# A gate/up stage in which one product gets its own PSUM banks and the weight sums are made in smaller pieces

## The chip, the core and the metric

The kernel runs on one core of a Trainium2 chip. The metric is the device time of one execution in microseconds (us). Engines are named PE (matrix multiply), DVE (vector), ACT (scalar), POOL and SP (which issues most transfers).

## The reference, cut to what matters here

One transformer block on 512 tokens of width 2048, in float32: a normed input projection, three mixers (a delta-rule recurrence, a gated linear recurrence, chunked retention), an output projection with residual, and a gated feed-forward block. The change lies in the last of these:

```python
h = rms_norm(x, norm2_g[l])
x = x + (jax.nn.silu(h @ ffn_w_gate[l]) * (h @ ffn_w_up[l])) @ ffn_w_down[l]
return rms_norm(x, final_norm_g)
```

The inner width is 5632.

## The kernel before

Every float32 product is made of three passes: each operand is split into a high half and the rest, and `mm3` (L161) runs high·high, high·low and low·high (L162 to L164) into the same PSUM bank. `split` (L157) makes the two halves: ACT casts the high half (L158), DVE subtracts it from the raw value (L141, through `tt`) for the low half.

The kernel does the input projection and the mixers (to about 750 us), the output projection (to about 925), the gate/up stage (to about 1827) and the down projection (to the end). The normed activation lies in SBUF as split pieces (`form(...)`: HH, HL, FAH, FAL).

The gate/up stage runs 11 units (`gate_up`, L993 to L1059). A unit multiplies the activation with four blocks of weights, b11, b21, b12 and b22, each of two buffers of 128 x 2048 (b11 = RB0, RB1; b12 = RB2, RB3; b21 = RB4, RB5; b22 = RB6 and RAW), loaded on SP's queue (L998). It uses a scheme with seven products on sums of blocks in place of eight on blocks. A `product` (L1001) has four pieces of 1024 weight columns; a piece is split into one of three slots (WH/WL twice, a part of HH/HL once) and used by 12 matmuls of 128x512. The products go into pairs of PSUM banks: bA is banks 0 and 1, bB is 2 and 3, bC is 4 and 5. The order of a unit:

1. b11 into bA, copied to E; then b11 becomes b11 + b12
2. b21 added into bA, whose result goes through tanh to G; then b12 becomes b12 + b22
3. b12 (the sum) into bB
4. b11 (the sum) into bC; then b11 becomes b11 + b22
5. b11 (the new sum) into bA; then E, H and X are formed from bA, bB and bC on DVE, and b21 becomes b21 + b11
6. b21 (the sum) into bB, from which H is subtracted, and which goes through tanh
7. b22 added into bC; E and G are finished

Each sum is made by `block` (L1013): two DVE additions of 128x2048. Then 16 transposes (L1056) go through banks 6 and 7; ACT copies them out (L1058) and stores them to HBM (`hscr`, L1059) from its own queue. High priority (`hp_`) lets the scheduler place such work early, among the matmuls of the next unit.

The down projection loads those activations back (`load_h`, L1100, on SP's queue, L1105), splits them (GH, GLo), and loads its weights in pieces of 128x512 (`wpieces`, L1085, transfers at L1093) into the buffers RAW and RW2.

The order of the instructions on each engine comes from the tile scheduler, which follows the order of the program and the priorities; a transfer is issued when its buffer and its queue slot are free, in the order of its queue.

Of the kernel before, what the change touches and what calls it, by code (L numbers as in the profile page):

```python
# [12 lines left out]
AF = mybir.ActivationFunctionType  # L13
# [18 lines left out]
NU = DFF // 512  # L32
# [66 lines left out]
def hybrid_block(ctx: ExitStack, tc: tile.TileContext, A: dict, out: bass.AP, dbg=None):  # L99
    nc = tc.nc  # L100
    V, S, G, PE = nc.vector, nc.scalar, nc.gpsimd, nc.tensor
# [17 lines left out]
    bank = [pp.tile([128, 512], F32, name=f"bank{i}") for i in range(8)]  # L119
# [9 lines left out]
    hscr = dp.tile([NCT, 128, T], F32, name="hscr")  # L129

    def c(name):
        o, n = CO[name]
        return cst[:, o:o + n] if o < NC1 else cs2[:, o - NC1:o - NC1 + n]
# [6 lines left out]
    def tt(o, a, b, op, eng=None):  # L140
        (eng or V).tensor_tensor(out=o, in0=a, in1=b, op=op)  # L141
# [7 lines left out]
    def stt(o, a, s, b, op0, op1, **kw):  # L149
        V.scalar_tensor_tensor(out=o, in0=a, scalar=s, in1=b, op0=op0, op1=op1, **kw)  # L150

    def act(o, a, f, scale=1.0, bias=0.0, **kw):
        S.activation(out=o, in_=a, func=f, scale=scale, bias=bias, **kw)  # L153

    MUL, ADD, SUB, MAX, MIN = ALU.mult, ALU.add, ALU.subtract, ALU.max, ALU.min

    def split(raw, hi, lo):  # L157
        S.copy(out=hi, in_=raw)  # L158
        tt(lo, raw, hi.bitcast(F32), SUB)

    def mm3(o, wh, wl, xh, xl, first, last, **kw):  # L161
        PE.matmul(o, wh, xh, start=first, stop=False, **kw)  # L162
        PE.matmul(o, wh, xl, start=False, stop=False, **kw)  # L163
        PE.matmul(o, wl, xh, start=False, stop=last, **kw)  # L164
# [13 lines left out]
    def sl(i, n=1):  # L178
        i -= (i > 9) + (i > 33) + (i > 44)
        return M[:, i * 512:(i + n) * 512]  # L180
# [10 lines left out]
    def nxt(k, n):  # L191
        v = ring[k]
        ring[k] = (v + 1) % n
        return v
# [27 lines left out]
    def head_rsqrt_stat(sq, rhs, n, mmb, floor=None, eps=None, kn=None):  # L222
        nt = sq.shape[-1] // 128
        v, y, h, t = smalls(nt * n, kn)
        b = mmb()
        for i in range(nt):
            mm(b[:, i * n:(i + 1) * n], sq[:, i * 128:(i + 1) * 128], rhs)
        if eps is None:
            ts(v, b[:, 0:nt * n], floor, MAX)
        else:  # L230
            ts(v, b[:, 0:nt * n], eps, ADD)
        rsqrt(y, v, (h, t))
        return y
# [36 lines left out]
    def proj(name, j, between=None):  # L270
        idx = W_IDX[(name, j)]
        o = bank[1 if ring["cv"] else nxt("proj", 2)]
        for half in range(2):
            with tc.high_priority() if idx > 1 else ExitStack():
                r = RAW[:, nxt("raw", 2), :]
                nc.sync.dma_start(out=r, in_=A["w_in"][idx, half])
                pcs = []
                for u in range(2):
                    w = nxt("w", 4)
                    split(r[:, u * 512:(u + 1) * 512], WH[:, w, :], WL[:, w, :])  # L280
                    pcs.append(w)
            if half and between:
                between()
            for u in range(2):
                w = pcs[u]
                for kk in range(4):
                    k = half * 8 + u * 4 + kk
                    cs = slice(kk * 128, (kk + 1) * 128)
                    mm3(o, WH[:, w, cs], WL[:, w, cs], HH[:, k, :], HL[:, k, :], k == 0, k == KT - 1)
        return o  # L290

    tok = []
    first = proj("k", 0, lambda: tok.append(head_rsqrt_stat(acc, c("mD"), 1, mmb, eps=NORM_EPS)))
# [350 lines left out]
    xc, tr, ti, la, th, lt, gx, g2 = (sl(34 + i) for i in range(8))  # L644
# [262 lines left out]
    E_, H_, X_, G_ = (ap_.tile([128, 2, T], F32, name=n) for n in ("E", "H", "X2", "G1"))  # L907
# [3 lines left out]
    def form(hl, j):  # L911
        if j < NFA:
            return (FAH, FAL)[hl][:, j, :, :]
        i = (j - NFA) * 1792
        return (HH, HL)[hl].rearrange("p k t -> p (k t)")[:, i:i + 1792].rearrange("p (f t) -> p f t", f=7)

    def fslot(i):
        if i < 2:
            return tuple(w[:, 2 * i:2 * i + 2, :].rearrange("p a b -> p (a b)") for w in (WH, WL))
        return tuple(w.rearrange("p k t -> p (k t)")[:, 7168:8192] for w in (HH, HL))  # L920
# [30 lines left out]
    for n, (ct, q) in enumerate(O_PIECES):  # L951
# [10 lines left out]
        if q == 3:  # L962
            b, x1 = ob[ct]
# [22 lines left out]
    rh, r2h = drv[:, 0:4], drv[:, 4:8]  # L986
# [6 lines left out]
    def gate_up(u):  # L993
        b11, b21, b12, b22 = blocks
        with tc.high_priority():
            for t_, m, half in ((b11, 0, 0), (b21, 0, 1), (b12, 1, 0), (b22, 1, 1)):
                for i in range(2):
                    nc.sync.dma_start(out=t_[i], in_=A["w_gu"][u, m, half, i])  # L998
        bA, bB, bC = (bank[0], bank[1]), (bank[2], bank[3]), (bank[4], bank[5])

        def product(raw, f, bs, first):  # L1001
            for jj in range(4):
                wh, wl = fslot(nxt("fs", 3))
                with tc.high_priority():
                    split(raw[jj // 2][:, 1024 * (jj % 2):1024 * (jj % 2) + 1024], wh, wl)
                for t in range(2):
                    tk = slice(128 * t, 128 * t + 128)
                    for i in range(2):
                        j, cs = 2 * jj + i, slice(512 * i, 512 * i + 512)
                        mm3(bs[t], form(0, j)[:, f, tk], form(1, j)[:, f, tk], wh[:, cs], wl[:, cs],  # L1010
                            first and j == 0, j == 7, skip_group_check=not first)

        def block(o, a, b_):  # L1013
            with tc.high_priority():
                for i in range(2):
                    tt(o[i], a[i], b_[i], ADD)

        two = range(2)
        hp_ = tc.high_priority
        product(b11, 0, bA, True)  # L1020
        with hp_():
            for t in two:
                S.copy(out=E_[:, t, :], in_=bA[t])
        block(b11, b11, b12)
        product(b21, 1, bA, False)
        with hp_():
            for t in two:
                act(G_[:, t, :], bA[t], AF.Tanh, scale=rh[:, t:t + 1])
                stt(G_[:, t, :], G_[:, t, :], 1.0, bA[t], ADD, MUL)
        block(b12, b12, b22)  # L1030
        product(b12, 4, bB, True)
        product(b11, 3, bC, True)
        block(b11, b11, b22)
        product(b11, 5, bA, True)
        with hp_():
            for t in two:
                tt(E_[:, t, :], bA[t], E_[:, t, :], SUB)
                tt(H_[:, t, :], bB[t], E_[:, t, :], ADD)
                tt(X_[:, t, :], bC[t], H_[:, t, :], ADD)
        block(b21, b21, b11)  # L1040
        product(b21, 2, bB, True)
        with hp_():
            for t in two:
                tt(H_[:, t, :], bB[t], H_[:, t, :], SUB)
                act(bB[t], H_[:, t, :], AF.Tanh, scale=rh[:, 2 + t:3 + t])
                stt(H_[:, t, :], bB[t], 1.0, H_[:, t, :], ADD, MUL)
                stt(X_[:, t, :], H_[:, t, :], r2h[:, 2 + t:3 + t], X_[:, t, :], MUL, MUL)
        product(b22, 6, bC, False)
        with hp_():
            for t in two:  # L1050
                tt(E_[:, t, :], bC[t], E_[:, t, :], ADD)
                stt(G_[:, t, :], G_[:, t, :], r2h[:, t:t + 1], E_[:, t, :], MUL, MUL)
            for f in range(4):
                b = bank[6 + nxt("tr", 2)]
                for t in range(4):
                    PE.transpose(b[:, 128 * t:128 * t + 128], (G_, X_)[t // 2][:, t % 2, 128 * f:128 * f + 128], ident)  # L1056
                st = H_[:, nxt("st", 2), :]
                S.copy(out=st, in_=b)  # L1058
                S.dma_start(out=hscr[4 * u + f], in_=st)  # L1059

    for u in range(NU):
        gate_up(u)
# [37 lines left out]
    def load_h(ci, n):  # L1100
        for i, ct in enumerate(range(D_START[ci], D_START[ci] + n)):
            f = FT[:, nxt("ft", 4), :]
            slot = ct % NS
            with tc.high_priority():
                nc.sync.dma_start(out=f, in_=hscr[ct])  # L1105
                split(f, GH[slot], GLo[slot])

    def down(ci, n):
# [118 lines left out]
    def lastb():  # L1227
        return bank[nxt("last", 2)]

    load_h(0, CHUNKS[0])  # L1230
    for ci, n in enumerate(CHUNKS):
        if ci < len(CHUNKS) - 1:
# [118 lines left out]
```

## Time and profile before

| what | value |
|---|---|
| median of 3 runs | 2339.6 us (2338.05 to 2344.82) |
| profiled execution | 2344.13 us |
| its span | 2342.3 us |
| PE busy | 2270.9 us, 97% of the span |
| DVE busy | 1627.8 us, 69% |
| ACT busy | 1000.3 us, 43% |
| mean granted clock of the PE | 0.99 |
| chain of work that ended last | PE 82%, DVE 11%, issue 4%, ACT 2%, DMA 1% |

The span is the profiled program from its first to its last instruction; the time of the run is 1.8 us more. Matmuls overlap, so that a busy PE shows durations longer than the distance of two starts. A wait in a row stands in brackets: the idle time of the engine before the instruction, and what ended it. The granted clock is 1.00 at 2.4 GHz and 0.50 at 1.2 GHz.

### The profile page before, as it was taken

How to read it: one execution, taken by the hardware profiler on the slowest of the kernel's cores; microseconds unless marked ns; L12 is line 12 of the kernel's file. 1: busy time of each engine (PE TensorE's matmuls, PEld its weight loads, DVE VectorE, ACT ScalarE, POOL GpSimd, SP SyncE). 2: the span in 40 equal slices, each digit the busy share in tenths (PEclk: the TensorE clock that was granted, in tenths of full speed). 3: DMA queues.
4: the chain of work that ended last, by engine and by line, in shares of the span. 5: the costliest groups of instructions: out<-in, count | busy, mean ns of one | idle time of the engine just before them, and what ended most of it. 6: DMA issues, size and time to landing. Idle time of an engine off the chain costs nothing.

```text
span 2342.3 us, 29241 instructions
## 1 busy us (share of the span) xinstructions
PE 2270.9 (97%) x11005; PEld 1859.6 (79%) x11005; DVE 1627.8 (69%) x2661; ACT 1000.3 (43%) x1646; POOL 22.0 (1%) x59
## 2 busy tenths in 40 slices
PE   9999999999999999999999999999999799999998
PEld 7878778778788888777877777787777688888887
DVE  7788699687556546877777877777787455565555
ACT  5563464454235434344444344444434432232234
POOL 0000000000000000000000000000000000000000
PEclk9999999999989999999999999999999899999999
DMA  5324233333323554333423332342330554444332
GB/s 198 101 81 118 72 100 84 106 93 103 97 73 104 186 165 162 110 106 117 152 92 119 115 117 99 117 153 90 126 109 19 176 153 131 135 150 134 115 106 73
DMA packets 119070, 272.51 MB, mean 116 GB/s; under 512 B 35904, under 2 KB 42304, under 8 KB 107536
## 3 DMA queue, kind: packets, MB, share of 16 engines
q1 hardware_dynamic: 108208, 250.46, 33.8%
q10 hardware_dynamic: 8448, 12.59, 1.4%
q0 software_dynamic: 2272, 7.58, 1.1%
q8 instruction: 87, 1.43, 0.3%
q14 instruction: 55, 0.45, 0.1%
HBM read 241.36 MB, written 27.66 MB: 115 GB/s over the span
## 4 chain that ended last, share of the span: by engine, by line
PE 82%; DVE 11%; issue 4%; ACT 2%; DMA 1%; SPq 0%; ACTq 0%; DVEq 0%
PE bank L163 25%; PE bank L162 25%; PE bank L164 25%; PE bank L167 5%; DVE WL L141 3%; DVE RB L141 2%; DVE M L141 1%; ACT WH L158 1%; PE bank L573 1%; DVE E L141 1%; DVE HL L141 1%; PE bank L1056 1%; PE bank L596 1%; DVE M L150 0%; ACT HH L158 0%
## 5 line engine op out<-in xcount | busy, mean ns | idle before, releaser
L158 ACT CAST WH<-RAW 128x512 fp32r<-128x512 f32 (+1 forms) x335 | 214.1, 640 | 416.5 <-PE bank L163 360.8
L162 PE MATMUL bank<-HH,WH 128*128 128x512 f32 x928 | 370.5, 399 | 8.8 <-ACT HH L153 5.8
L164 PE MATMUL bank<-HH,WL 128*128 128x512 f32 x928 | 368.3, 397 | 0.0
L163 PE MATMUL bank<-HL,WH 128*128 128x512 f32 x928 | 367.8, 396 | 0.0
L141 DVE TENSOR_TENSOR WL<-RAW,WH 128x512 fp32r<-128x512 f32 (+1 forms) x335 | 237.5, 710 | 130.5 <-ACT WH L158 126.7
L158 ACT CAST WH<-RB 128x1024 fp32r<-128x1024 f32 x191 | 201.1, 1053 | 291.4 <-PE bank L164 283.1
L141 DVE TENSOR_TENSOR WL<-RB,WH 128x1024 fp32r<-128x1024 f32 x191 | 232.3, 1221 | 131.4 <-ACT WH L158 130.8
L162 PE MATMUL bank<-GH,WH 128*128 128x512 f32 x640 | 251.0, 393 | 10.5 <-ACT WH L158 10.5
L163 PE MATMUL bank<-GLo,WH 128*128 128x512 f32 x640 | 250.5, 391 | 0.0
L164 PE MATMUL bank<-GH,WL 128*128 128x512 f32 x640 | 250.4, 391 | 0.0
L163 PE MATMUL bank<-WL,HH 128*128 128x512 f32 (+1 forms) x604 | 219.1, 363 | 7.8 <-DVE WL L141 7.8
L141 DVE TENSOR_TENSOR X<-X,bank 128x512 f32<-128x512 f32 (+1 forms) x178 | 115.7, 655 | 156.7 <-PE bank L164 156.0
L162 PE MATMUL bank<-WH,HH 128*128 128x512 f32 (+1 forms) x604 | 215.9, 360 | 1.3 <-ACT WH L158 1.3
L164 PE MATMUL bank<-WH,HL 128*128 128x512 f32 (+1 forms) x604 | 216.8, 359 | 0.0
L162 PEld LDWEIGHTS bank<-HH,WH 128*128 128x128 f32 x928 | 175.5, 189 | 46.0 <-ACT HH L153 5.8
L164 PEld LDWEIGHTS bank<-HH,WL 128*128 128x128 f32 x928 | 175.4, 189 | 36.2 <-issue 1.4
L163 PEld LDWEIGHTS bank<-HL,WH 128*128 128x128 f32 x928 | 175.6, 189 | 35.5 <-issue 1.4
L141 DVE TENSOR_TENSOR HL<-RB,HH 128x1024 fp32r<-128x1024 f32 (+1 forms) x123 | 125.9, 1038 | 72.7 <-ACT HH L158 72.3
L162 PE MATMUL bank<-WH,FAH 128*128 128x512 f32 x412 | 162.2, 394 | 11.0 <-DVE H L141 11.0
L158 ACT CAST HH<-RB 128x1024 fp32r<-128x1024 f32 x95 | 99.9, 1052 | 147.7 <-PE bank L164 145.9
L163 PE MATMUL bank<-WL,FAH 128*128 128x512 f32 x412 | 160.5, 390 | 0.0
L164 PE MATMUL bank<-WH,FAL 128*128 128x512 f32 x412 | 160.5, 391 | 0.0
(239 smaller groups left out, 3839.3 us busy)
## 6 DMA issues: line engine op xcount, KB each, us to landing
RB<-in_w_gu_dram SPq DMA_DIRECT2D x77, 1024.0 KB, 4.8
RAW<-in_w_in_dram SPq DMA_DIRECT2D x76, 512.0 KB, 3.7
RAW<-in_w_dn_dram SPq DMA_DIRECT2D x96, 256.0 KB, 2.6
RW<-in_w_dn_dram SPq DMA_DIRECT2D x80, 256.0 KB, 2.6
RAW<-in_w_out_dram SPq DMA_DIRECT2D x32, 512.0 KB, 3.6
RAW<-in_w_gu_dram SPq DMA_DIRECT2D x11, 1024.0 KB, 4.9
hscr<-H ACTq DMA_DIRECT2D x44, 256.0 KB, 2.2
FT<-hscr SPq DMA_DIRECT2D x44, 256.0 KB, 3.3
```

The costliest lines, as they stand in the source:

```text
L141: (eng or V).tensor_tensor(out=o, in0=a, in1=b, op=op)
L158: S.copy(out=hi, in_=raw)
L162: PE.matmul(o, wh, xh, start=first, stop=False, **kw)
L163: PE.matmul(o, wh, xl, start=False, stop=False, **kw)
L164: PE.matmul(o, wl, xh, start=False, stop=last, **kw)
L167: PE.matmul(o, l, r, start=start, stop=stop)
L573: PE.matmul(F[:, q, hv[e]], LS[e][:, ch, :], VS[:, ch, hv[e]], start=(q == 0 and e == 0), stop=True, skip_group_check=(q > 0 or e > 0))
L596: PE.matmul(F[:, q, :], P_[q][1][:, ch, :], ZBq[:, q, :], start=False, stop=True, skip_group_check=True)
L1056: PE.transpose(b[:, 128 * t:128 * t + 128], (G_, X_)[t // 2][:, t % 2, 128 * f:128 * f + 128], ident)
```

## The change

- A fourth pair of banks, bD (6 and 7), takes the sixth product of a unit; the transposes move to bB (2 and 3).
- `block` is gone. `product` takes a pair of blocks and adds, behind the split of each piece, the 1024 columns of that piece. The sum b11 + b12 is made in product 1, b12 + b22 in product 2, b11 + b22 in product 4 and b21 + b11 in product 5.
- In the last unit the transposes, copies and stores have no high priority. The first loads of activations for the down projection are issued by ACT, not SP.

```diff
--- before.py
+++ after.py
@@ -996,13 +996,18 @@
             for t_, m, half in ((b11, 0, 0), (b21, 0, 1), (b12, 1, 0), (b22, 1, 1)):
                 for i in range(2):
                     nc.sync.dma_start(out=t_[i], in_=A["w_gu"][u, m, half, i])
-        bA, bB, bC = (bank[0], bank[1]), (bank[2], bank[3]), (bank[4], bank[5])
-
-        def product(raw, f, bs, first):
+        bA, bB, bC, bD = ((bank[i], bank[i + 1]) for i in (0, 2, 4, 6))
+
+        def piece(b_, jj):
+            return b_[jj // 2][:, 1024 * (jj % 2):1024 * (jj % 2) + 1024]
+
+        def product(raw, f, bs, first, add=None):
             for jj in range(4):
                 wh, wl = fslot(nxt("fs", 3))
                 with tc.high_priority():
-                    split(raw[jj // 2][:, 1024 * (jj % 2):1024 * (jj % 2) + 1024], wh, wl)
+                    split(piece(raw, jj), wh, wl)
+                    if add:
+                        tt(piece(add[0], jj), piece(add[0], jj), piece(add[1], jj), ADD)
                 for t in range(2):
                     tk = slice(128 * t, 128 * t + 128)
                     for i in range(2):
@@ -1010,48 +1015,40 @@
                         mm3(bs[t], form(0, j)[:, f, tk], form(1, j)[:, f, tk], wh[:, cs], wl[:, cs],
                             first and j == 0, j == 7, skip_group_check=not first)
 
-        def block(o, a, b_):
-            with tc.high_priority():
-                for i in range(2):
-                    tt(o[i], a[i], b_[i], ADD)
-
         two = range(2)
         hp_ = tc.high_priority
-        product(b11, 0, bA, True)
+        product(b11, 0, bA, True, (b11, b12))
         with hp_():
             for t in two:
                 S.copy(out=E_[:, t, :], in_=bA[t])
-        block(b11, b11, b12)
-        product(b21, 1, bA, False)
+        product(b21, 1, bA, False, (b12, b22))
         with hp_():
             for t in two:
                 act(G_[:, t, :], bA[t], AF.Tanh, scale=rh[:, t:t + 1])
                 stt(G_[:, t, :], G_[:, t, :], 1.0, bA[t], ADD, MUL)
-        block(b12, b12, b22)
         product(b12, 4, bB, True)
-        product(b11, 3, bC, True)
-        block(b11, b11, b22)
-        product(b11, 5, bA, True)
+        product(b11, 3, bC, True, (b11, b22))
+        product(b11, 5, bA, True, (b21, b11))
         with hp_():
             for t in two:
                 tt(E_[:, t, :], bA[t], E_[:, t, :], SUB)
                 tt(H_[:, t, :], bB[t], E_[:, t, :], ADD)
                 tt(X_[:, t, :], bC[t], H_[:, t, :], ADD)
-        block(b21, b21, b11)
-        product(b21, 2, bB, True)
+        product(b21, 2, bD, True)
         with hp_():
             for t in two:
-                tt(H_[:, t, :], bB[t], H_[:, t, :], SUB)
-                act(bB[t], H_[:, t, :], AF.Tanh, scale=rh[:, 2 + t:3 + t])
-                stt(H_[:, t, :], bB[t], 1.0, H_[:, t, :], ADD, MUL)
+                tt(H_[:, t, :], bD[t], H_[:, t, :], SUB)
+                act(bD[t], H_[:, t, :], AF.Tanh, scale=rh[:, 2 + t:3 + t])
+                stt(H_[:, t, :], bD[t], 1.0, H_[:, t, :], ADD, MUL)
                 stt(X_[:, t, :], H_[:, t, :], r2h[:, 2 + t:3 + t], X_[:, t, :], MUL, MUL)
         product(b22, 6, bC, False)
         with hp_():
             for t in two:
                 tt(E_[:, t, :], bC[t], E_[:, t, :], ADD)
                 stt(G_[:, t, :], G_[:, t, :], r2h[:, t:t + 1], E_[:, t, :], MUL, MUL)
+        with hp_() if u < NU - 1 else ExitStack():
             for f in range(4):
-                b = bank[6 + nxt("tr", 2)]
+                b = bB[nxt("tr", 2)]
                 for t in range(4):
                     PE.transpose(b[:, 128 * t:128 * t + 128], (G_, X_)[t // 2][:, t % 2, 128 * f:128 * f + 128], ident)
                 st = H_[:, nxt("st", 2), :]
@@ -1102,7 +1099,7 @@
             f = FT[:, nxt("ft", 4), :]
             slot = ct % NS
             with tc.high_priority():
-                nc.sync.dma_start(out=f, in_=hscr[ct])
+                (nc.sync if ci else S).dma_start(out=f, in_=hscr[ct])
                 split(f, GH[slot], GLo[slot])
 
     def down(ci, n):
```

The scheduler's order moves with it. In the rows below, RB0_6002, RB1_6003, RB2_6004, RB3_6005, RB4_6006, RB5_6007, RB6_6008 and RAW_76 are the weight buffers, WL_78 and HL_80 the low halves of a split, E_6011 and G1_6014 the activations' buffers (G's second half is the later of its two rows), and a row with RB or RAW on both sides of the arrow and 128x1024 or 128x2048 is a sum.

DVE at the boundary of two units, from the split of the second piece of the new unit's first weight buffer, before:

```order
L141 TENSOR_TENSOR WL_78<-RB0_6002,WH_77 128x1024
L141 TENSOR_TENSOR E_6011<-bank4_85,E_6011 128x512
L141 TENSOR_TENSOR RB0_6002<-RB0_6002,RB2_6004 128x2048
L150 SCALAR_TENSOR_TENSOR G1_6014<-G1_6014,drv_71,E_6011 128x512
L141 TENSOR_TENSOR RB2_6004<-RB2_6004,RB6_6008 128x2048
L141 TENSOR_TENSOR WL_78<-RB1_6003,WH_77 128x1024
L141 TENSOR_TENSOR HL_80<-RB1_6003,HH_79 128x1024
L141 TENSOR_TENSOR WL_78<-RB4_6006,WH_77 128x1024
L141 TENSOR_TENSOR RB1_6003<-RB1_6003,RB3_6005 128x2048
L141 TENSOR_TENSOR WL_78<-RB4_6006,WH_77 128x1024
L141 TENSOR_TENSOR RB3_6005<-RB3_6005,RAW_76 128x2048
L141 TENSOR_TENSOR HL_80<-RB5_6007,HH_79 128x1024
```

And now, from the split of the first piece:

```order
L141 TENSOR_TENSOR HL_80<-RB0_6002,HH_79 128x1024
L141 TENSOR_TENSOR RB0_6002<-RB0_6002,RB2_6004 128x1024
L141 TENSOR_TENSOR RB2_6004<-RB2_6004,RB6_6008 128x1024
L141 TENSOR_TENSOR E_6011<-bank4_85,E_6011 128x512
L141 TENSOR_TENSOR WL_78<-RB0_6002,WH_77 128x1024
L150 SCALAR_TENSOR_TENSOR G1_6014<-G1_6014,drv_71,E_6011 128x512
L141 TENSOR_TENSOR WL_78<-RB1_6003,WH_77 128x1024
L141 TENSOR_TENSOR E_6011<-bank5_86,E_6011 128x512
L141 TENSOR_TENSOR RB0_6002<-RB0_6002,RB2_6004 128x1024
L141 TENSOR_TENSOR HL_80<-RB1_6003,HH_79 128x1024
L141 TENSOR_TENSOR RB1_6003<-RB1_6003,RB3_6005 128x1024
L141 TENSOR_TENSOR WL_78<-RB4_6006,WH_77 128x1024
```

Seven rows further on, behind four more sums, stands the row that finishes G's second half; before it stood two rows after the last one shown. The sums of 2048 columns, four in the stretch, have become pieces that begin between the splits.

DVE at the start of the first unit, behind the last output projection (G1 + bank5), where HL rows of 128x256 split the activation out of RB3 to RB6, before:

```order
L141 TENSOR_TENSOR HL_80<-RB4_6006,HH_79 128x256
L141 TENSOR_TENSOR HL_80<-RB5_6007,HH_79 128x256
L141 TENSOR_TENSOR HL_80<-RB6_6008,HH_79 128x256
L141 TENSOR_TENSOR G1_6014<-G1_6014,bank5_86 128x512
L141 TENSOR_TENSOR WL_78<-RB0_6002,WH_77 128x1024
L141 TENSOR_TENSOR HL_80<-RB1_6003,HH_79 128x1024
L141 TENSOR_TENSOR RB0_6002<-RB0_6002,RB2_6004 128x2048
L141 TENSOR_TENSOR WL_78<-RB1_6003,WH_77 128x1024
L141 TENSOR_TENSOR E_6011<-E_6011,H_6012 128x512
L141 TENSOR_TENSOR WL_78<-RB4_6006,WH_77 128x1024
L141 TENSOR_TENSOR RB3_6005<-RB3_6005 128x512
L141 TENSOR_TENSOR HL_80<-RB3_6005,HH_79 128x256
```

And now, beginning four rows behind the same row of G1:

```order
L141 TENSOR_TENSOR WL_78<-RB1_6003,WH_77 128x1024
L141 TENSOR_TENSOR E_6011<-E_6011,H_6012 128x512
L141 TENSOR_TENSOR RB3_6005<-RB3_6005 128x512
L141 TENSOR_TENSOR HL_80<-RB3_6005,HH_79 128x256
L141 TENSOR_TENSOR RB3_6005<-RB3_6005 128x256
L141 TENSOR_TENSOR HL_80<-RB3_6005,HH_79 128x256
L141 TENSOR_TENSOR RB3_6005<-RB3_6005 128x256
L141 TENSOR_TENSOR HL_80<-RB3_6005,HH_79 128x256 x3
L141 TENSOR_TENSOR HL_80<-RB4_6006,HH_79 128x256
L141 TENSOR_TENSOR HL_80<-RB5_6007,HH_79 128x256
L141 TENSOR_TENSOR HL_80<-RB6_6008,HH_79 128x256
L141 TENSOR_TENSOR HL_80<-RB3_6005,HH_79 128x256
```

The last readers of RB4, RB5 and RB6 as activation (the rows `HL_80<-RB4_6006,HH_79 128x256` and its two neighbours) stood ahead of the output projection's sum and stand now behind the work on RB3; the transfers that fill these buffers with weights wait for them.

ACT at the end of the stage, from the last store of a transposed tile on (FT is the raw activation of the down projection, GH its high half, RAW and RW2 its raw weights, WH and WH2 their high halves), before:

```order
L1059 DMA hscr_97<-H_6012 128x512
L158 CAST WH2_12183<-RAW_76 128x512 x3
L158 CAST GH0_12173<-FT_12181 128x512
L158 CAST GH2_12177<-FT_12181 128x512
L158 CAST WH_77<-RW2_12184 128x512 x3
L158 CAST GH4_12187<-FT_12181 128x512
L158 CAST GH6_12191<-FT_12181 128x512
L158 CAST WH_77<-RW2_12184 128x512
L158 CAST GH3_12179<-FT_12181 128x512
```

And now:

```order
L1056 DMA hscr_97<-H_6012 128x512
L1102 DMA FT_12269<-hscr_97 128x512 x4
L158 CAST WH2_12271<-RAW_76 128x512 x2
L158 CAST WH_77<-RW2_12272 128x512 x2
L158 CAST GH1_12263<-FT_12269 128x512
L158 CAST WH_77<-RW2_12272 128x512
L158 CAST GH3_12267<-FT_12269 128x512
L158 CAST WH_77<-RW2_12272 128x512
L158 CAST GH2_12265<-FT_12269 128x512
L158 CAST WH2_12271<-RAW_76 128x512
L158 CAST GH0_12261<-FT_12269 128x512
```

Four loads of activations stand now in ACT's queue behind the stores, and the cast of GH0, with which the first matmul of the down projection begins, is the last of eleven casts; before, it was the fourth.

## Rows read from the trace of the kernel before

**Rows 1.** The page, part 1: busy time of each engine, share of the span, instructions.

```profile
PE 2270.9 (97%) x11005; PEld 1859.6 (79%) x11005; DVE 1627.8 (69%) x2661; ACT 1000.3 (43%) x1646; POOL 22.0 (1%) x59
```

**Rows 2.** Waits of PE, 1027 to 1830 us: who waited for what; us, times, longest.

```profile
PE bank L162 <- DVE H L141: 15.7, 10, 1.6
PE bank L163 <- DVE WL L141: 6.2, 12, 0.7
PE bank L163 <- DVE HL L141: 3.1, 6, 0.7
PE bank L1056 <- DVE G L150: 1.2, 2, 0.9
```

**Rows 3.** Windows, one unit: length, busy PE, PEld, DVE, ACT, POOL; PEclk, DMA share, GB/s.

```profile
1555.50:1637.30 81.80, 79.22 (x353) 64.24 (x352) 62.22 (x54) 35.06 (x39) 0.00 (x0) 1.00 0.34 116
```

**Rows 4.** Timeline of PE where product 6 starts: start, duration, line, operation [idle before].

```profile
1557.56 0.39 PE L163 MATMUL bank<-HL,HH 128*128 128x512 f32 x1
1557.79 0.39 PE L164 MATMUL bank<-HH,HL 128*128 128x512 f32 x1
1559.74 0.47 PE L162 MATMUL bank<-WH,FAH 128*128 128x512 f32 x1 [1.57 <-DVE H L141]
```

**Rows 5.** Timeline of DVE at the same place.

```profile
1557.72 1.28 DVE L141 TENSOR_TENSOR E<-bank,E 128x512 f32<-128x512 f32 x2
1558.92 0.68 DVE L141 TENSOR_TENSOR H<-bank,E 128x512 f32<-128x512 f32 x1
```

**Rows 6.** Timeline of PE in the first two products of the next unit.

```profile
1588.23 0.50 PE L163 MATMUL bank<-WL,HH 128*128 128x512 f32 x1 [0.32 <-DVE WL L141]
...
1597.17 0.50 PE L163 MATMUL bank<-HL,HH 128*128 128x512 f32 x1 [0.70 <-DVE HL L141]
```

**Rows 7.** Timeline of DVE in the same stretch.

```profile
1580.15 1.23 DVE L141 TENSOR_TENSOR WL<-RB,WH 128x1024 fp32r<-128x1024 f32 x1 [1.45 <-ACT WH L158]
...
1593.70 2.28 DVE L141 TENSOR_TENSOR RB<-RB,RAW 128x2048 f32<-128x2048 f32 x1
1595.90 1.21 DVE L141 TENSOR_TENSOR HL<-RB,HH 128x1024 fp32r<-128x1024 f32 x1
1597.04 0.68 DVE L141 TENSOR_TENSOR E<-bank,E 128x512 f32<-128x512 f32 x1
1597.75 0.75 DVE L150 SCALAR_TENSOR_TENSOR G<-G,drv,E 128x512 f32<-128x512 f32 x1
```

**Rows 8.** Timeline of SP's queue: weight loads of the first unit and, last, of a later one.

```profile
925.53 1.28 SPq L998 DMA_DIRECT2D RB<-in_w_gu_dram  x3
...
944.34 14.01 SPq L998 DMA_DIRECT2D RB<-in_w_gu_dram  x3
...
1570.52 0.33 SPq L998 DMA_DIRECT2D RB<-in_w_gu_dram  x1
```

**Rows 9.** Timeline of PE and windows (columns as rows 3), third product, first unit.

```profile
955.65 0.73 PE L162 MATMUL bank<-WH,HH 128*128 128x512 f32 x2 [1.32 <-ACT WH L158]
...
955.00:960.00 5.00, 3.83 (x9) 2.76 (x10) 3.56 (x4) 2.49 (x3) 0.00 (x0) 0.70 0.23 33
```

**Rows 10.** Timeline of PE at the start of the down projection.

```profile
1837.32 1.31 PE L162 MATMUL bank<-GH,WH 128*128 128x512 f32 x2 [6.23 <-ACT WH L158]
...
1845.89 0.80 PE L162 MATMUL bank<-GH,WH 128*128 128x512 f32 x1 [4.29 <-ACT WH L158]
...
1851.25 0.41 PE L164 MATMUL bank<-GH,WL 128*128 128x512 f32 x1
```

**Rows 11.** Timeline of ACT's queue: the last store of the stage.

```profile
1833.68 0.33 ACTq L1059 DMA_DIRECT2D hscr<-H  x1
```

**Rows 12.** The page, part 6: transfers, issuing queue, count, size, median us to landing.

```profile
RB<-in_w_gu_dram SPq DMA_DIRECT2D x77, 1024.0 KB, 4.8
...
RW<-in_w_dn_dram SPq DMA_DIRECT2D x80, 256.0 KB, 2.6
...
hscr<-H ACTq DMA_DIRECT2D x44, 256.0 KB, 2.2
```

## The prediction

> **What bounds the kernel now.** I read the page first, then the waits of the PE over the gate/up stage, then one unit of that stage by windows, and then the timeline around each wait. The PE is busy 97% of the span [rows 1], so a change pays only where the PE stands still or runs at its lower clock. In the stretch that holds the boundaries between the eleven units, the PE waits 15.7 us in ten pieces for the H subtraction, 6.2 and 3.1 us in eighteen pieces for low halves of split weights, and 1.2 us for G [rows 2]. A unit takes 81.80 us with the PE busy 79.20 at clock 1.00, and DVE busy 62.22 [rows 3]: DVE is not full, it is late at certain places.
>
> Place one, the start of the fourth sum's product: matmuls follow each other every 0.23 us, then one starts 1.95 us after its neighbour, 1.57 of it waiting for H [rows 4]. DVE is then working through two E subtractions and one H subtraction, which empty banks 0 to 3 after the product before; H ends at 1559.60 and the PE restarts at 1559.74 [rows 5]. Place two, the first product of a unit: the PE waits 0.32 us for a low half and later 0.70 us [rows 6]. DVE does the subtractions in order, and a 2048-column sum stands ahead of the late one: 2.28 us long, the next start 2.20 us later [rows 7].
>
> **The change, part by part.**
>
> *Own banks for the product.* The new product writes banks 6 and 7, whose last readers are long done, so its first matmul waits only for its own split. What goes at each unit: 1.95 − 0.23 = 1.72 us, and some 0.08 us because the first matmul after a stall runs 0.08 us longer than the others [rows 4]; 1.80 us × 11 units = **19.8 us**. The E, H and X subtractions still run on DVE but nothing on the PE waits for them before the seventh product, 10.9 us (48 × 0.227) later. In exchange, the transposes move to banks 2 and 3, and product three must follow ACT's copies out of them. In the shifted times of the trace the last copy ends 1 to 2 us before product three wants its bank, so I put this at nothing; without that cover the cost would be the missing part of one 2.2 us store [rows 12], since a copy waits for a staging buffer.
>
> *Sums in pieces.* Sixteen 1024-column sums replace eight of 2048. A 1024-column subtraction occupies 1.14 us of DVE and a 2048-column sum 2.20 [rows 7], so one sum costs 2 × 1.14 − 2.20 = 0.08 us more, 0.6 us in a unit with some 19 us of DVE idle. VectorE: DVE Perf Modes in the Trainium skill (section Side-by-side: where the cycles go) gives every instruction a fixed term of about 150 cycles beside its length, an estimate of 0.16 us at its 0.96 GHz; by it a unit's eight extra sums take 1.25 us, twice the rows' price, and the gain below would shrink by up to half of that at each boundary. The rows decide.
>
> The gain lies in the order. As the rows of the order show, a split no longer has more than two 1024-column sums ahead of it there, and the first sums start in the hole of 1.45 us that DVE now spends waiting for a cast [rows 7]. Laying the new DVE rows end to end with 1.14 us for each 1024-column instruction, 0.6 to 0.75 us for each 512-column one, the two low halves arrive in time: the first by over 2 us, the second just about. That removes 0.32 and 0.70 us plus about 0.15 us of slow restart each, some 1.4 us a unit. What is late next is the second half of G: eight pieces of sum (9.1 us) now stand before it where four whole sums (8.8 us) stood [rows 7]; it ends about 1.2 us earlier than now, while the PE arrives 1.4 us earlier. I price that wait at 0.3 to 0.6 us, taken 0.45. Net 0.95 × 10 boundaries, less some units where the second stall is short: **7.5 us**, between 0 (all of it returns at G) and 12 (nothing does, 9.3 us of waits and 2.7 of restarts [rows 2]).
>
> *Start of the first unit, which gets worse.* The rows of the order show that the last piece of the activation split from buffer RB4 now stands behind the work on RB3. The load into RB4 waits for it. Before, three loads were issued at 925.53 and the next only at 944.34, after the cast of the third sum was late and the PE lost 1.32 us and then ran at a mean clock of 0.70 for 5 us, a mix of its two levels of 2.4 and 1.2 GHz [rows 8, 9]: 1.3 + 0.3 × 5 = 2.8 us. With the new order the first of the loads goes out around 935.5 to 936, lands 4.8 us later [rows 12], and its cast and subtraction take two more: the PE wants the second product around 937.7 and gets its weights at 941.5 to 942.5. I put this at 4.3 us of standing still and 1.7 us at the lower clock, minus the 2.8 us that the later place then no longer costs: **+3 us**, between −1 (loads at the fastest, old stall gone) and +6 (both).
>
> *End of the stage.* The last unit's transposes and stores keep their place, the first activations of the down projection are loaded through ACT's queue, and the weights' loads no longer queue on SP behind them. Now the first down matmul starts at 1837.32 after 6.23 us of waiting, there is a second wait of 4.29 us before 1845.89, and the half clock lasts to 1851.25 [rows 10]. New: ACT issues the last store at 1833.68 [rows 11], it lands 2.2 us later, a weight load that waits for that store's queue slot needs 2.6 us more [rows 12], then four 0.6 us casts and one 0.7 us subtraction end at about 1842. After that all of the first chunk is at hand: 24 matmuls, of which some ten at the lower clock cost 0.2 us more each, bring the PE to where it stood at 1851.5 by about 1842 + 5.4 + 2 = 1849.5. **−2 us**, between +1 (DVE's eleven subtractions end at 1843.5, slow clock longer) and −6 (the last load earlier). DMA: Bandwidth & Descriptors in the Trainium skill (section Issuing engines are not separate DMA queues) says that issuing from a second engine saves only the issuing time; by it this part would give 0. The trace's second wait, for a load that stands late in the queue's order, is such time.
>
> **Sum.** −19.8 − 7.5 + 3 − 2 = −26.3 us. The profiled execution took 2344.1 us (2342.3 of span, 1.8 around it), 4.5 above the median of the three runs. 2344.1 − 26.3 = 2317.8; by the median, 2339.6 − 26.3 = **2313 us**.
>
> **The rivals.** A: *DVE stays the bound at the boundary.* If the waits for the low halves only move to G and to the next split, 7.5 us fall to 0: 2339.6 − 19.8 + 3 − 2 = 2321 us. For it: DVE has as much to do there as before. Against it: the hole it now fills. Chance 0.17. The fixed term of the VectorE page would lead here too, the part of it that the rows above do not show.
>
> B: *both ends go badly.* The load delay of the first unit costs its upper bound and the end gains nothing: 2339.6 − 27.3 + 6 + 1 = 2319; with A, 2327. Chance 0.06 beside A. The rule of the DMA page would give the end of this one.
>
> C, slower: *the early sum waits for its weights.* The third DVE row of a boundary now reads RB6, which before was read some 2 us later, and on DVE every split queues behind it. RB6 is issued at 1570.52 [rows 8], 11 us before the boundary's first matmul, and loads land after 4.8 us [rows 12], 6 us ahead. Only if it landed later than 12 us would the PE wait, 1 us for each us at ten boundaries; to turn −26 into +7 it must be 3.3 us later still, over 15 us. Chance 0.03: nothing in the trace is near it, since the same loads go out at the same places.
>
> D: *the change does not do what it says*, the wait for H merely becoming one for the split of the same product, which stands behind H on DVE: 2339.6 − 7.5 + 1 = 2333 or, with nothing left, 2340. The new order puts that split ahead of the E and H subtractions. Chance 0.04.
>
> **The numbers.** The forecast has 0.70. The low end is all 12 us of part two, −1 at the first unit and −4 at the end: 2339.6 − 19.8 − 12 − 1 − 4 = 2303. The high end is A with B, 2327. About 0.3% (7 us) is what a measurement of this kernel tells from no change, so faster means under 2332.6: the forecast, A, B give 0.92, and I keep 0.02 of it for what I have not seen: 0.90. Within 0.3%: most of D and a part of what is unseen, 0.06. Slower: C and a rest, 0.04.
>
> **What would show it.** Right: the wait on H is gone in every unit, a unit takes 78.5 to 79.5 us in place of 81.80, transposes wait for G up to 0.6 us each unit; the second product of the first unit starts 4 us late, while the wait before the third is gone; the first down matmul starts later after the last transpose than before, and no second wait follows. Wrong: a unit at 80 us with waits for low halves (A), long waits on RB6's sum (C), or H's wait under a new name (D).

## The result, and the profile after

The changed kernel takes 2310.8 us (median of 4 runs, 2310.1 to 2315.2), the kernel before 2338.8 us (4 runs, 2337.9 to 2344.8). The ratio is 0.9879 with a 95% interval of 0.9858 to 0.9900: 28.0 us less. The forecast was 2313 us.

The profiled execution has a span of 2308.2 us, 34.1 us less than the one of before. Not all of that is the change. Ahead of gate/up the PE runs the same matmuls in the same order in both programs, and the last of them started at 925.35 us before and at 920.54 after. Most of these 4.8 us is an unlucky piece in the trace of before, told in the last section; without them the spans differ by 29.3 us.

The waits of the PE from 1027 to 1805 us, which leaves out the first unit and its boundary as [rows 2] do, changed kernel (who waited for what: us, times, longest):

```profile
PE bank L1053 <- DVE G L150: 4.2, 11, 1.0
PE bank L1053 <- ACT H L1055: 0.3, 1, 0.3
```

Of the four groups of [rows 2], three are gone: the 15.7 us for H and the 9.3 us for low halves. What is left is G, 1.2 us before, all of it at the last transposes, and 4.2 now. One unit by windows (columns as in [rows 3]):

```profile
1555.00:1633.83 78.83, 78.49 (x353) 64.39 (x352) 62.78 (x63) 35.05 (x39) 0.00 (x0) 1.00 0.36 120
```

78.83 us in place of 81.80, with the PE busy for all but 0.34 us of it. DVE has 63 instructions in this window in place of 54 and 0.56 us more work (62.22 before).

The start of the sixth product, timeline of PE, where [rows 4] had 1.95 us from one start to the next:

```profile
1534.85 0.39 PE L164 MATMUL bank<-HH,HL 128*128 128x512 f32 x1
1535.08 0.39 PE L162 MATMUL bank<-WH,FAH 128*128 128x512 f32 x1
```

0.23 us, no wait. DVE at the boundary of two units, timeline, to be held against [rows 7]:

```profile
1552.72 1.23 DVE L141 TENSOR_TENSOR HL<-RB,HH 128x1024 fp32r<-128x1024 f32 x1 [0.60 <-ACT HH L158]
1553.98 2.48 DVE L141 TENSOR_TENSOR RB<-RB,RB 128x1024 f32<-128x1024 f32 x2
...
1560.52 1.21 DVE L141 TENSOR_TENSOR RB<-RB,RB 128x1024 f32<-128x1024 f32 x1
...
1569.62 1.22 DVE L141 TENSOR_TENSOR HL<-RB,HH 128x1024 fp32r<-128x1024 f32 x1
1570.75 1.22 DVE L141 TENSOR_TENSOR RB<-RB,RAW 128x1024 f32<-128x1024 f32 x1
1571.89 0.74 DVE L150 SCALAR_TENSOR_TENSOR G<-G,drv,E 128x512 f32<-128x512 f32 x1
```

Two pieces of sum fill the hole in which DVE waited for a cast, and from then to G's second half it has no idle time. G ends at 1572.63; the transposes that wait for it, in the timeline of PE for two units, one row each:

```profile
1493.85 0.33 PE L1053 MATMUL bank<-cst,G 128*128 128x128 f32 x1 [0.34 <-DVE G L150]
...
1572.69 0.33 PE L1053 MATMUL bank<-cst,G 128*128 128x128 f32 x1 [0.34 <-DVE G L150]
```

The start of the first unit, where [rows 8, 9] showed loads at 925.53 and a wait at the third product: timeline of SP's queue, timeline of PE, and a window.

```profile
930.57 1.98 SPq L998 DMA_DIRECT2D RB<-in_w_gu_dram  x4
```

```profile
936.33 0.73 PE L162 MATMUL bank<-WH,FAH 128*128 128x512 f32 x2 [3.31 <-ACT WH L158]
937.59 0.79 PE L163 MATMUL bank<-WL,FAH 128*128 128x512 f32 x1 [0.52 <-DVE WL L141]
```

```profile
935.00:940.00 5.00, 3.15 (x8) 2.23 (x9) 3.52 (x3) 3.04 (x3) 0.00 (x0) 0.76 1.00 424
```

Ten microseconds after the last matmul of the output projection the loads go out, and the wait has moved from the third product to the second and grown from 1.32 to 3.31 us. The clock falls as before: 0.76 is a mean of its two levels, 2.4 and 1.2 GHz.

The end of the stage, first the down projection's first matmul, to be held against [rows 10], then ACT's queue and the chain of waits:

```profile
1810.22 1.65 PE L162 MATMUL bank<-GH,WH 128*128 128x512 f32 x3 [12.78 <-ACT GH L158]
```

```profile
1800.43 2.30 ACTq L1102 DMA_DIRECT2D FT<-hscr  x4
```

```profile
1801.45 4.95 DMA FT<-hscr
```

The last row is the one of the four loads that ended ACT's wait, from issue to landing. One wait of 12.78 us stands in place of 6.23 and 4.29.

By stretches of the two traces: from the last matmul of the output projection to the first of the second unit 83.65 us before and 84.47 after, which is +2.6 once the 1.80 us of the sixth product are taken out; the other ten units, up to the ninth of the last unit's transposes, −29.7; from there to the end of the span −0.5, called the end below. With −1.8 for the first unit's sixth product the sum is −29.4, the 29.3 us of the spans within rounding.

### The profile page after: what moved, and what is told of

The parts are those of the page before. It is cut to its first block, busy times and chain, and to the rows that moved or that the text cites. A ratio compares the mean times of both kernels' runs of the same rounds, so it can differ in the third digit from the quotient of the medians.

```text
span 2308.2 us, 29340 instructions
## 1 busy us (share of the span) xinstructions
PE 2255.6 (98%) x11005; PEld 1855.7 (80%) x11005; DVE 1633.9 (71%) x2749; ACT 1000.1 (43%) x1646; POOL 22.0 (1%) x59
## 4 chain that ended last, share of the span: by engine, by line
PE 81%; DVE 14%; ACT 2%; issue 2%; DMA 1%; ACTq 0%; DVEq 0%; SPq 0%
PE bank L162 25%; PE bank L163 25%; PE bank L164 25%; PE bank L167 4%; DVE RB L141 4%; DVE WL L141 3%; DVE M L141 1%; DVE HL L141 1%; PE bank L573 1%; PE bank L1053 1%; DVE G L150 1%; DVE E L141 1%; PE bank L596 1%; ACT WH L158 1%; DVE M L150 1%
## 5 line engine op out<-in xcount | busy, mean ns | idle before, releaser
L141 DVE TENSOR_TENSOR RB<-RB,RB 128x1024 f32<-128x1024 f32 x132 | 160.1, 1220 | 2.0
```

## The experiments

Eight kernels ran, in two groups of four. Medians of the kernel before beside them: 2338.1 us (11 runs) for the first four, 2339.3 us (7 runs) for the others. Since one run differs from the next by some 5 us through a stretch that no kernel here touches, the lengths of stretches are the finer measure. The length of a unit is the distance from one unit's transposes to the next unit's.

**The own banks alone.**

```diff
-        bA, bB, bC = (bank[0], bank[1]), (bank[2], bank[3]), (bank[4], bank[5])
+        bA, bB, bC, bD = ((bank[i], bank[i + 1]) for i in (0, 2, 4, 6))
...
-        product(b21, 2, bB, True)
+        product(b21, 2, bD, True)
...
-                tt(H_[:, t, :], bB[t], H_[:, t, :], SUB)
-                act(bB[t], H_[:, t, :], AF.Tanh, scale=rh[:, 2 + t:3 + t])
-                stt(H_[:, t, :], bB[t], 1.0, H_[:, t, :], ADD, MUL)
+                tt(H_[:, t, :], bD[t], H_[:, t, :], SUB)
+                act(bD[t], H_[:, t, :], AF.Tanh, scale=rh[:, 2 + t:3 + t])
+                stt(H_[:, t, :], bD[t], 1.0, H_[:, t, :], ADD, MUL)
...
-                b = bank[6 + nxt("tr", 2)]
+                b = bB[nxt("tr", 2)]
```

> The kernel before with the own bank pair alone: the sixth product goes into banks 6 and 7, the transposes into 2 and 3; the sums stay whole and in their old places, the end of the stage stays as it was. My theory (the wait on H is worth 1.80 us a unit by itself, whatever the sums do): 2338.8 - 19.8 = 2319 us, a unit of 80.0 us, no wait of the PE on H, the waits for low halves of 0.32 and 0.70 us still there. Rival (DVE is late at the boundary all the same, so that a product that starts earlier only meets its next split later): the waits for low halves grow by up to 1.8 us a unit, the unit stays between 80.5 and 81.8 us and the time between 2326 and 2338 us.

Measured: 2318.6 us (4 runs, ratio 0.9908, 0.9890 to 0.9927). Waits of the PE for DVE in its whole gate/up stage, and the timeline of PE at two boundaries:

```profile
PE bank L163 <- DVE WL L141: 7.7, 15, 0.7
PE bank L163 <- DVE HL L141: 3.1, 6, 0.7
PE bank L1056 <- DVE G L150: 1.2, 2, 0.9
```

```profile
1420.20 0.33 PE L1056 MATMUL bank<-cst,G 128*128 128x128 f32 x1
...
1500.16 0.33 PE L1056 MATMUL bank<-cst,G 128*128 128x128 f32 x1
```

A unit of 79.96 us, 1.84 less than before. No group for H. The waits for low halves are what they were: [rows 2] leave out the first unit and its boundary, and in the same stretch this kernel has 6.1 and 3.1 us. The rival falls: nothing is given back at the boundary. The first unit of this trace is 3.4 us shorter than before, 1.8 by the sixth product and 1.6 by luck: the clock didn't fall after the wait at its third product, as it had before [rows 9].

**The sums in pieces alone.** The changed kernel with bB again for the sixth product, banks 6 and 7 for the transposes, and the end of the stage as before.

> The sums in pieces alone: the changed kernel with the sixth product back in banks 2 and 3, the transposes in 6 and 7 and the end of the stage as before. My theory (the pieces take away the two waits for low halves, 1.17 us a unit, and the late loads of the first unit cost 2.6 us): 2338.8 - 11.7 + 2.6 = 2329.7 us, a unit of 80.6 us, a wait on H of 1.57 us in each unit. Rival (pieces only help once the product has its own banks, since DVE must first get through E and H): a unit of 81.8 us, 2339 us or more with the first unit's loss, 2341 us.

Measured: 2332.2 us (8 runs, 2330.9 to 2335.6; ratio 0.9971, 0.9961 to 0.9982). Waits of the PE for DVE in its gate/up stage, and two boundaries:

```profile
PE bank L162 <- DVE H L141: 17.3, 11, 1.6
PE bank L1053 <- DVE G L150: 4.6, 12, 1.0
PE bank L163 <- DVE HL L141: 0.6, 1, 0.6
```

```profile
1431.33 0.33 PE L1053 MATMUL bank<-cst,G 128*128 128x128 f32 x1 [0.34 <-DVE G L150]
...
1512.01 0.33 PE L1053 MATMUL bank<-cst,G 128*128 128x128 f32 x1 [0.34 <-DVE G L150]
```

A unit of 80.68 us, 1.12 less than before, with H waited for as ever. The two parts don't need each other: 1.84 + 1.12 = 2.96 us, and the whole change has 81.80 − 78.83 = 2.97. The time is 2.5 us over what I expected. The profiled execution is one of those with the long piece ahead of the stage; behind that, its trace is 9.3 us shorter than the one of before, where I expected 9.1: ten units −11.2, the first unit +3.3, the end −1.4.

**The end of the stage as before.**

```diff
-        with hp_() if u < NU - 1 else ExitStack():
+        with hp_():
...
-                (nc.sync if ci else S).dma_start(out=f, in_=hscr[ct])
+                nc.sync.dma_start(out=f, in_=hscr[ct])
```

> The changed kernel with its third part undone: the last unit's transposes have high priority again, and the first activations of the down projection are loaded on SP's queue. My theory (the third part gained 0.5 us in the traces: one long wait in place of two): 2311.3 us, the first down matmul after some 6 us of waiting and a second wait of 4 us. Rival (the third part carries a share of the gain, up to 6 us): 2314 to 2317 us. Second rival (it costs, since the loads stand behind the stores): 2308 us.

Measured: 2311.8 us (4 runs; ratio 0.9879, 0.9862 to 0.9895), 1.0 over the changed kernel and within the spread of the runs. The timeline of PE has the two waits back:

```profile
1805.01 1.31 PE L162 MATMUL bank<-GH,WH 128*128 128x512 f32 x2 [6.22 <-ACT WH L158]
...
1814.03 0.80 PE L162 MATMUL bank<-GH,WH 128*128 128x512 f32 x1 [4.41 <-ACT WH L158]
```

The end takes 512.7 us here, 511.9 in the changed kernel and 512.4 in the kernel before. That is no more than the spread of one and the same code: with the end as before it takes 511.0 (the sums in pieces alone) to 512.8 us (the own banks alone), with the third part 511.8 to 512.3 in the four runs that leave it as it is. A gain of the third part isn't shown; it can hardly be more than a microsecond.

**Whole sums in the new places.**

```diff
-                    if add:
-                        tt(piece(add[0], jj), piece(add[0], jj), piece(add[1], jj), ADD)
+                    if add and jj % 2:
+                        tt(add[0][jj // 2], add[0][jj // 2], add[1][jj // 2], ADD)
```

> The changed kernel with sums of 2048 columns at the second and fourth piece of the same four products, in place of 1024 columns at each. If the place of the sums is what counts (no two sums ahead of a split), the unit stays at 78.8 us, and the first unit starts as before because the scheduler keeps the old order there: 2310.8 - 2.6 = 2308 us. If the size of the pieces counts, the waits for low halves come back with 0.3 to 1.2 us a unit: a unit of 79.2 to 80 us, 2312 to 2320 us.

Measured: 2322.5 us (4 runs, 2317.5 to 2322.9; ratio 0.9920, 0.9901 to 0.9939). Timeline of DVE at a boundary, and of PE where it waits for the last of these rows:

```profile
1493.75 1.21 DVE L141 TENSOR_TENSOR WL<-RB,WH 128x1024 fp32r<-128x1024 f32 x1
1494.88 2.28 DVE L141 TENSOR_TENSOR RB<-RB,RAW 128x2048 f32<-128x2048 f32 x1
1497.09 0.74 DVE L150 SCALAR_TENSOR_TENSOR G<-G,drv,E 128x512 f32<-128x512 f32 x1
```

```profile
1418.04 0.33 PE L1053 MATMUL bank<-cst,G 128*128 128x128 f32 x1 [1.44 <-DVE G L150]
...
1497.88 0.33 PE L1053 MATMUL bank<-cst,G 128*128 128x128 f32 x1 [1.43 <-DVE G L150]
```

The three other runs took 2322.2 to 2322.9 us and the profiled one 2317.5, so the median is above both ranges. Behind the output projection this trace is 6.2 us longer than the changed kernel's: ten units +10.2, the first unit −4.4, the end +0.4. Where the three other runs lost 5 us more isn't known, since they have no trace.

A unit of 79.84 us: both ideas were half right. The waits for low halves in the boundaries stay away, so the place of the sums is enough for those. But a whole sum stands ahead of G, and the wait for G is 1.44 us in place of 0.34. That is where the size of a piece counts.

**G ahead of three sums.** The sums of the second product at normal priority:

```diff
-                    if add:
+                    if add and f != 1:
                         tt(piece(add[0], jj), piece(add[0], jj), piece(add[1], jj), ADD)
+                if add and f == 1:
+                    tt(piece(add[0], jj), piece(add[0], jj), piece(add[1], jj), ADD)
```

> The changed kernel with the sums of the second product (b12 + b22) at normal priority, so that in the order of DVE the second half of G stands ahead of three of the boundary's eight pieces of sum and of two splits. My theory (what is left at the boundary is G behind the sums, 0.34 us of waiting a unit and some slow restart): no wait on G, a unit of 78.3 to 78.5 us, 2310.8 - 4 = 2307 us. Rival (DVE is full there; what G gains the next split loses): waits for low halves of 0.3 us or more a unit, 2311 us or more.

Measured: 2305.3 us (4 runs, 2302.9 to 2309.0; ratio 0.9856, 0.9839 to 0.9873), 5.5 less than the changed kernel. Waits of the PE for DVE in the stage, all of them in the first unit or at the last transposes, and two boundaries:

```profile
PE bank L1055 <- DVE G L150: 1.2, 2, 0.9
PE bank L163 <- DVE WL L141: 0.5, 1, 0.5
```

```profile
1408.04 0.27 PE L1055 MATMUL bank<-cst,G 128*128 128x128 f32 x1
...
1486.30 0.27 PE L1055 MATMUL bank<-cst,G 128*128 128x128 f32 x1
```

A unit of 78.26 us, 0.57 less, with no wait for low halves in exchange and no wait of the PE left at a boundary. G was the last late thing there, as the theory has it, and DVE is not full. Its wait cost 0.57 us a unit, though only 0.34 us of that is idle time of the PE.

**Whole sums in the first unit alone.**

```diff
-                    if add:
+                    if add and u:
                         tt(piece(add[0], jj), piece(add[0], jj), piece(add[1], jj), ADD)
+                    elif add and jj % 2:
+                        tt(add[0][jj // 2], add[0][jj // 2], add[1][jj // 2], ADD)
```

> The changed kernel with whole sums in the first unit alone, at the second and fourth piece. There the scheduler keeps the old order: the last readers of RB4, RB5 and RB6 as activation stand ahead of the output projection's sum, and the weight loads go out some 5 us earlier. My theory (the first unit lost 2.6 us through these loads): 2310.8 - 2.6 = 2308 us, the second product starts without its wait of 3.3 us. Rival (the wait only goes from the second product to the third, where it was before): 2310 to 2312 us. The unit of the steady stretch stays at 78.8 us.

Measured: 2308.1 us (4 runs, 2307.4 to 2314.7; ratio 0.9873, 0.9853 to 0.9892), 2.7 less. Timelines of SP's queue and of PE:

```profile
922.14 1.28 SPq L998 DMA_DIRECT2D RB<-in_w_gu_dram  x3
```

```profile
952.21 0.73 PE L162 MATMUL bank<-WH,HH 128*128 128x512 f32 x2 [1.25 <-ACT WH L158]
953.47 0.50 PE L163 MATMUL bank<-WL,HH 128*128 128x512 f32 x1 [0.53 <-DVE WL L141]
```

The loads go out 0.2 us after the last matmul of the output projection (921.97), the wait of 3.3 us at the second product is gone, and the third has its 1.25 us back. From the last matmul of the output projection to the second unit it takes 80.15 us in place of 84.47. So the pieces cost 4.3 us in the first unit of the traces. The medians differ by 2.7, within the variation of the stretch ahead, from which this profiled execution came 1.4 us later. The first unit takes 80.0 to 80.3 us in the four kernels with the old order there and the sixth product in its own banks, and 83.8 to 85.3 in the four with pieces and own banks.

**The first activations through POOL's queue.**

```diff
-                (nc.sync if ci else S).dma_start(out=f, in_=hscr[ct])
+                (nc.sync if ci else nc.gpsimd).dma_start(out=f, in_=hscr[ct])
```

> The changed kernel with the first activations of the down projection loaded on POOL's queue, which is empty there. They no longer stand behind ACT's stores, and the weight loads on SP get queue slots that do not wait for these stores. My theory (the 12.8 us of waiting before the first down matmul are made by the loads behind the stores, 4.95 us from issue to landing, and the eleven casts behind them): the first down matmul starts some 6 us earlier after the last transpose, 2310.8 - 6 = 2305 us. Rival (ACT is the bound there, its copies and casts one after the other): 2308 to 2311 us.

Measured: 2307.2 us (4 runs, 2304.3 to 2309.4; ratio 0.9858, 0.9839 to 0.9878). Timelines of POOL and of PE:

```profile
1745.28 2.12 POOL L1102 DMA_DIRECT2D FT<-hscr  x4 [998.61 <-DVE WL L141]
```

```profile
1809.18 0.80 PE L162 MATMUL bank<-GH,WH 128*128 128x512 f32 x1 [5.69 <-ACT GH L158]
1810.23 0.80 PE L163 MATMUL bank<-GLo,WH 128*128 128x512 f32 x1 [0.26 <-DVE GLo L141]
```

The four loads go out at 1745.28 us, 54 us ahead of the last unit's first transposes; in ACT's queue they went out behind the transposes and the stores. Two things moved with them: all eight of the first weight loads on SP's queue go out by 1797.7 us, where two of them stood until 1798.98 and 1803.22 behind the stores, and the first cast of an activation is the fifth of ACT's casts. What each of the three is worth alone was not tried. 5.69 us of waiting stand in place of 12.78, and the second wait of the kernel before (4.29 us) doesn't come back. The end takes 505.3 us against 511.9, 6.6 less. ACT has the same copies and casts to do, so the rival, ACT as the bound, falls. The median shows 3.6 of it; the fastest runs differ by 5.8 (2304.3 and 2310.1), and the stage ahead ended late in the profiled run.

**The three together.**

> The three edits of the runs before this one together: sums of the second product at normal priority, whole sums in the first unit, POOL loads at the end of the stage. They lie in different stretches, so I expect their sum: 2310.8 - 4 - 2.6 - 6 = 2298 us. If one of them only shifts a wait, its share is missing: 2301 to 2305 us.

Measured: 2294.0 us (4 runs, 2292.7 to 2294.9; ratio 0.9806, 0.9791 to 0.9820), 16.7 less than the changed kernel. Waits of the PE in the stage:

```profile
PE bank L162 <- ACT GH L158: 5.7, 1, 5.7
PE bank L1057 <- DVE G L150: 1.3, 3, 0.9
PE bank L162 <- ACT WH L158: 1.2, 1, 1.2
```

By the traces: ten units −5.5, since one boundary waited for G once and its unit took 78.5 us in place of 78.26; the first unit 80.14 us, −4.3; the end 504.9 us, −7.0; the sum is −16.8. The edits lie in different stretches, and their gains add up: each alone was −5.7, −4.3 and −6.6 in its stretch. This version beats both kernels.

## Why the prediction was right

- *Own banks, −19.8.* Right in mechanism and size: with nothing else changed 79.96 us a unit, 1.84 less, and 2318.6 us where the term alone gives 2319. Ten units are 18.2 us shorter in that trace, and the first unit's sixth product adds 1.8. The price of the moved transposes, put at nothing, is nothing: no product waits for a copy out of banks 2 and 3.
- *Sums in pieces, −7.5.* The mechanism held, the size was too small: ten units lost 11.2 us (the sums alone) to 11.5 us (the change against the own banks alone), next to the end of my range that I had called "nothing returns" (12). Two steps failed, by some 2 us each. One is the discount, from 9.5 to 7.5, for units in which the second stall is short: there are none, since the nine distances from one unit's start to the next are 78.80 to 78.84 us. The other is the price of the waits. From 79.96 us a unit with both waits for low halves to 78.26 with no wait at all it is 1.70 us, where I had 1.4: the restart behind a wait costs more than the 0.15 us I took. G's wait costs 0.57 of it, where I had 0.45, so that 1.13 was left and not 0.95. That the price of a piece is small was right: DVE's work in a unit rose by 0.56 us (0.6 predicted), 0.07 us a sum. By an estimate from the fixed term in VectorE: DVE Perf Modes in the Trainium skill (section Side-by-side: where the cycles go) it would have been 1.25 us; the measured 0.56 is under half of that and decides.
- *Start of the first unit, +3.* Right against the trace of before: +2.6, through the wait that was named, at the product that was named. The loads went out 10.0 us after the last matmul of the output projection, which is 935.4 on the clock of the trace before; I had said 935.5 to 936. Here luck helped. I subtracted 2.8 us for the old wait with its lower clock; of the five executions with such a wait at the third product the one of before is the only one in which the clock fell. Without that fall the first unit lies at 80.1 us, and against it the price is 4.3 us, which I saw only from the experiment.
- *End of the stage, −2.* Size −0.5, which is not clear of the spread of the end, so that the sign isn't shown either. I let the last weight load end the wait, at 2.6 us from issue to landing, and put the first matmul at 1842. It was the activation loads behind ACT's stores, the one that ended ACT's wait took 4.95 us, in a window (1801.0 to 1806.5) whose DMA share is 0.98, and seven casts followed, GH0's last. On the clock of the trace before, it landed at 1840.0 and the matmul started at 1843.9. No second wait followed, as forecast. The rule of DMA: Bandwidth & Descriptors in the Trainium skill (section Issuing engines are not separate DMA queues), that a second issuing engine saves only issuing time, gave 0 and was nearer here. The run with POOL's queue shows the other side: where the queue that is left has stores ahead of the loads and the new one has not, the end is 6.6 us shorter, with weight loads that go out earlier too.
- *Rival A* (DVE stays the bound) falls with the two runs of one part each, and with the run in which G moved ahead: a unit went to 78.26 us with more sums behind. *Rival C* (a sum waits for RB6) shows nowhere in the waits. *Rival D* (the change does not do what it says) falls with the missing wait on H. *Rival B* had one half: the end gained little or nothing.

Measured against the forecast, the change gained 0.2 us more at the sixth product, 0.4 at the first unit and 3.7 to 4.0 at the boundaries, and 1.5 less at the end; together the spans fell by 29.3 us where 26.3 were forecast, and the medians by 28.0. That the sum came so near owes something to errors of both signs. Two slips of the prediction change nothing: the chances of the forecast, of A and of B add up to 0.93, not 0.92, and the PE is busy for 79.22 us of a unit [rows 3], not 79.20.

## What to carry to other kernels

When an engine that is idle a quarter of the time still holds up another, read its order, not its load: look what stands between the late instruction and its inputs, cut that or move it behind, and price the next late instruction before summing up. A finer order can also move work in a stretch nobody looked at, here the first unit, where the last readers of a buffer fell behind other work and the loads that refill it with them. Small parts of a change are best measured by the stretch they touch; the medians showed a gain of 4.3 us in the first unit as 2.7.

## What the runs showed of the hardware that was not expected

The same wait can cost the clock or not. In the mixers the granted clock falls near 636 us in every profiled execution, while the PE has short pauses; windows of before and of the changed kernel:

```profile
640.00:650.00 10.00, 8.78 (x48) 7.50 (x46) 5.42 (x13) 3.58 (x15) 0.00 (x0) 0.50 0.01 2
650.00:660.00 10.00, 10.00 (x55) 8.34 (x54) 4.68 (x13) 2.54 (x8) 0.00 (x0) 0.67 0.00 1
```

```profile
640.00:650.00 10.00, 8.78 (x43) 7.63 (x42) 6.61 (x16) 2.65 (x10) 0.00 (x0) 0.63 0.01 2
650.00:660.00 10.00, 10.00 (x77) 8.87 (x78) 6.31 (x17) 3.96 (x11) 0.00 (x0) 1.00 0.00 1
```

With the same busy share, 8.78 and 10.00 us, the granted clock is 0.50 and 0.67 in one run and 0.63 and 1.00 in the other. By the traces' records of the granted clock the engine is at 1.2 GHz for 20.5 us before (636.1 to 656.6) and for 10.2 us in the changed kernel (637.2 to 647.5); in the eight other executions it is 13.7 us six times and 20.5 twice. Matched matmul by matmul, the trace of before lies 0.2 us behind the changed kernel's at 635 us, 1.3 at 645, and 4.8 from 655 us up to gate/up. In the ten profiled executions the last matmul of the output projection started between 920.54 and 925.75 us, a spread like the 5 us between single runs of one kernel. The same shows after the wait at the third product of the first unit: 1.32 us of it in the trace before with a clock of 0.70 behind it [rows 9], and 1.25 us in the run with whole sums in the first unit, with 1.00 in the windows from 950 to 955 and from 955 to 960 us. What decides between the two was not tried.
